# Loading streamed expert weights by whole thirds, into a ring of 15 places, three transfers under way

## Chip, cores and metric

The kernel runs on one core of one Trainium2 chip. The metric is the time of the program on the device in microseconds (us); lower is better. The times of a kernel are given as the median of its runs. One more execution is recorded by the hardware profiler, and all rows below come from that one.

## What is computed

One encoder layer over 1024 tokens of width 1024: windowed attention and a short gated convolution, joined by gates, then a mixture of 32 experts. Each token goes to one of four groups and there to two of eight experts. Only the last part concerns us here:

```python
def expert_block(args):
    xb, e = args
    hid = jax.nn.silu(xb @ w_gate[e]) * (xb @ w_up[e])
    return hid @ w_down[e]
...
y = y_pad[dest] * gates[order][:, None].astype(h.dtype)
out = jnp.zeros((t, d), h.dtype).at[tok].add(y)
```

The weights of one expert are 1024x256 (gate), 1024x256 (up) and 256x1024 (down) in float32, 3 MB, and 32 experts have 96 MB. All of them are used once.

## The kernel before

The program does norm, projections and attention, then the gates and the merge of both branches, then the experts. The experts' part (`phase_moe`, L1177 and after) takes the last 300 us of the span.

**An expert.** For expert e, GpSimd gathers up to 96 rows of the normed tokens from HBM into `xg` (L1121, an indirect DMA). TensorE turns them (`px`, L1132), ScalarE and VectorE split them into a high and a low part (`xT`), TensorE forms gate and up in one bank (`pgu`, 24 matmuls of 512 columns), ScalarE and VectorE form the hidden rows, TensorE turns them (`ph`, L1158) and multiplies by the down weights (`py`, 12 matmuls). ScalarE scales the result into `y` (L1170, two instructions), and GpSimd adds those rows to `out` in HBM (L1173, an indirect DMA that accumulates). There are two buffers `y`, the two halves of place 5, taken in turn; two `xg`; the accumulating transfers are ordered one behind the other, since they write the same tensor.

**The weights.** Host code lays them out as 96 thirds of 128 partitions x 2048 floats (1 MB, 8 KB a partition), numbered p = 0 to 95 in the order in which the kernel takes them: the gate and up weights are two thirds of an expert, its down weights the third one. A third has two halves s = 0, 1 (512 KB, 4 KB a partition). Each half, when it has come, is split once more, by ScalarE (L1107, high part) and VectorE (L1108, low part), into one of six places `wh` from which TensorE reads; `used()` issues these splits as TensorE lets go of a half. When VectorE has split a half, its place in the ring is free.

**The ring.** The first sixteen thirds (p below 16) are loaded whole or, for p = 12 and 13, as two halves into tiles of their own (`raw`), while merge and routing still run. From p = 16 on, the stream goes round the same memory. Thirds 16 and 17 go whole into places 2 and 0 (`WHOLE = 18`). From third 18 on, loads are halves into `slots`: the halves of places 2, 0, 1, 3, 4, 6, 7 to 15 in this order (place 5 serves as `y`) and one further half of its own, `more`, put in as number four, 31 halves in all. So a streamed half waits for the half 31 before it to be split, and by a dependency added by hand for the half four before it to have landed (`DEPTH = 4`): at most four halves, 2 MB, are under way. All loads are issued by SP's queue in order, but for the half (18, 1), which GpSimd's queue issues behind the gathers of experts 0 and 1 (`behind` only orders, it doesn't wait).

**Order.** ScalarE and VectorE run in the order of the program text in `phase_moe`: expert e's steps are woven with those of e - 1 and e + 1. The gather for expert e + 2 is issued when `xg` of expert e has been turned.

Of the kernel before, what the change touches and what calls it, by code (L numbers as in the profile page):

```python
# [8 lines left out]
F32 = mybir.dt.float32  # L9
# [8 lines left out]
P = 128  # L18
# [9 lines left out]
NE = 32  # L28
FF = 256
CAP = 96  # L30
LATE = (60, 94, 94)
WHOLE = 18
DEPTH = 4
TAP = 512
FILL = (4, 3, 4)

# [9 lines left out]
class Builder:  # L46
# [533 lines left out]

    def load(self, p, s=0):

        whole = p not in (12, 13) and p < WHOLE
        if (p, s) in self.loads:
            return
        if p in (0, 10, 14):
            pair = self.act(f"we{p}", {0: 3, 10: 4, 14: 1}[p], [2, 2048], F32)
            self.raw[p], self.raw[p + 1] = pair[:, 0], pair[:, 1]
        elif p in (12, 13):
            self.raw[p, s] = self.wpool.tile([P, 1024], F32, name=f"we{p}_{s}", tag="whl", bufs=4)  # L590
        elif p < 16 and p not in self.raw:
            tag = ("A0", "A1", "A2", "A3", "araw0", "craw0", "araw1", "craw1")[p - 2]
            self.raw[p] = (self.rawA if p < 6 else self.rawp).tile([P, 2048], F32, name=f"we{p}", tag=tag)
        elif p >= 16 and whole:
            self.raw[p] = self.raw[(2, 0)[p - 16]]
        j = self.order[p]
        to, sl = (self.raw[p], slice(0, 2048)) if whole else (self.half_of(p, s), slice(s * 1024, (s + 1) * 1024))
        q = self.nc.gpsimd if (p, s) == (18, 1) else self.nc.sync
        ins = q.dma_start(to, self.T["we"][j // 3, j % 3, :, sl])
        self.loads[p, s] = ins  # L600
        if whole:
            self.loads[p, 1] = ins
        if p == 15:
            self.behind(ins, self.wrote)
        if (p, s) == (18, 1):
            self.behind(ins, self.gathered)
        elif p > 18:
            dep = mybir.DependencyInfo(mybir.DependencyClass.Sync, mybir.DependencyReason.DATA)
            h = 2 * p + s - DEPTH
            self.tc.add_manual_dep(ins.ins, self.loads[h // 2, h % 2].ins.name, dep, reason="depth")  # L610

    def load_here(self, p):

# [2 lines left out]

    def half_of(self, p, s):

        if p in (12, 13):
            return self.raw[p, s]  # L620
        if p < 16:
            return self.raw[p][:, s * 1024:(s + 1) * 1024]
        return self.slots[(2 * p + s - 32) % len(self.slots)]

    def merge_consts(self, st):
        nc, T = self.nc, self.T
# [550 lines left out]
    def phase_moe(self, st):  # L1177
        nc, T = self.nc, self.T
        xp = self.pool("x6", stack=st)
        xts = [xp.tile([P, KT, 2, CAP], F32R, name="xT0")]  # L1180
        xgs = [xp.tile([P, D], F32, name=f"xg{i}") for i in range(2)]
        self.moe_pools(st, 0, 0)
        xts.append(self.sp6.tile([P, KT, 2, CAP], F32R, name="xT1"))
        for s in range(2):
            self.load(15, s)
        for s in range(2):
            self.half(1, s)
        self.nexth, self.free = 6, 0
        run = [self.expert(e, lambda c, s, e=e: self.w[3 * e + c, s], self.used, xgs[e % 2], xts[e % 2],
                           lambda e=e: self.slots[0] if e == NE - 1 else self.half_of(5, e % 2),  # L1190
                           self.idx[:CAP, 1, e:e + 1], self.gr[:CAP, 0, e:e + 1], self.gr[:CAP, 1, e:e + 1])
               for e in range(NE)]

        def start(e):
            next(run[e])
            if e + 2 < NE:
                self.gather(xgs[e % 2], self.idx[:CAP, 0, e + 2:e + 3])

        for e in range(2):
            self.gathered = self.gather(xgs[e], self.idx0[:CAP, e:e + 1])  # L1200
        order = [(p, s) for p in [2, 0, 1] + list(range(3, 16)) for s in range(2)]
        self.slots = [self.half_of(*h) for h in order if h[0] != 5]
        self.slots.insert(4, self.sp6.tile([P, 1024], F32, name="more"))
        for p in range(17, 19):
            for s in range(2):
                self.load(p, s)
        start(0)
        st.enter_context(self.tc.manual_schedule(engines={mybir.EngineType.Activation, mybir.EngineType.DVE}))
        for e in range(NE):
            next(run[e])  # L1210
            if e > 0:
                next(run[e - 1])
            if e + 1 < NE:
                start(e + 1)
            next(run[e])
            if e > 0:
                next(run[e - 1])
        next(run[-1])
        next(run[-1])
# [114 lines left out]
```

## Time and profile before

| | |
|---|---|
| Median of three runs | 977.77 us (977.6 to 978.74) |
| Profiled execution: its own time, its span | 980.05 us, 977.8 us |
| TensorE, busy share of the span | 97% (949.3 us) |
| VectorE, ScalarE, GpSimd | 75%, 60%, 12% |
| HBM read, written | 166.55 MB, 29.36 MB |
| DMA busy, last 12 of 40 slices | 9 tenths or more in 10 of them |
| Weight loads by SP's queue | 159 of 512 KB, 16 of 1024 KB |

The 40 slices of the page are 24.4 us each. TensorE shows nine tenths or more in nearly all of them, and so do the 16 DMA engines from slice 29 on, the experts' part. Shares over the whole span say little: the two meet only there, and the waits must be read by stretch. The DMA share of a stretch is the mean over 16 engines, and since transfers of neighbouring stretches are counted with where they start, it can read a few hundredths over 1.

### The profile page before, as it was taken

How to read it: one execution, taken by the hardware profiler on the slowest of the kernel's cores; microseconds unless marked ns; L12 is line 12 of the kernel's file. 1: busy time of each engine (PE TensorE's matmuls, PEld its weight loads, DVE VectorE, ACT ScalarE, POOL GpSimd, SP SyncE). 2: the span in 40 equal slices, each digit the busy share in tenths (PEclk: the TensorE clock that was granted, in tenths of full speed). 3: DMA queues.
4: the chain of work that ended last, by engine and by line, in shares of the span. 5: the costliest groups of instructions: out<-in, count | busy, mean ns of one | idle time of the engine just before them, and what ended most of it. 6: DMA issues, size and time to landing. Idle time of an engine off the chain costs nothing. (4 is left out here: it accounts for less than half of the span.)

```text
span 977.8 us, 13838 instructions
## 1 busy us (share of the span) xinstructions
PE 949.3 (97%) x4649; PEld 750.3 (77%) x4649; DVE 736.3 (75%) x1407; ACT 582.7 (60%) x1039; POOL 115.2 (12%) x90
## 2 busy tenths in 40 slices
PE   8999999999999999999999999979999999999993
PEld 5888888888878888888888888856777777777662
DVE  5777777878779656568765786478999999999882
ACT  4644555555544433346344435447999999899872
POOL 2222000000000000000000000013333232232211
PEclk9999999999999999999999999989999999999997
DMA  7201101000114233317677988768999999999993
GB/s 252 91 12 60 41 30 33 33 23 22 34 57 170 80 118 109 119 44 234 198 258 240 345 302 307 233 218 255 330 346 340 338 335 352 342 326 341 329 355 68
DMA packets 82749, 188.76 MB, mean 193 GB/s; under 512 B 10924, under 2 KB 28076, under 8 KB 80628
## 3 DMA queue, kind: packets, MB, share of 16 engines
q1 hardware_dynamic: 54772, 153.93, 45.3%
q0 software_dynamic: 7312, 17.60, 8.0%
q10 hardware_dynamic: 20592, 16.32, 5.0%
q8 instruction: 37, 0.61, 0.3%
q14 instruction: 36, 0.29, 0.1%
HBM read 166.55 MB, written 29.36 MB: 200 GB/s over the span
## 5 line engine op out<-in xcount | busy, mean ns | idle before, releaser
L1108 DVE TENSOR_TENSOR wh<-we,wh 128x1024 fp32r<-128x1024 f32 x186 | 219.8, 1217 | 29.7 <-ACT wh L1107 29.7
L1107 ACT ACTIVATE wh<-we 128x1024 fp32r<-128x1024 f32 x186 | 189.4, 1056 | 15.3 <-DMA we<-we 7.7
L70 PE MATMUL pgu<-wh,xT 128*96 128x512 f32 x768 | 190.5, 396 | 0.2 <-ACT xT L59 0.2
L70 PEld LDWEIGHTS pgu<-wh,xT 128*96 128x96 f32 x768 | 121.3, 161 | 49.9 <-ACT xT L59 0.4
L70 PE MATMUL py<-wh,hT 128*96 128x512 f32 x384 | 95.3, 395 | 3.8 <-DVE hT L60 2.0
L70 PEld LDWEIGHTS py<-wh,hT 128*96 128x96 f32 x384 | 61.4, 161 | 32.7 <-DVE hT L60 3.4
L70 PE MATMUL pc<-hT,wc_0s 128*128 128x512 f32 x288 | 77.5, 397 | 0.0
L70 PE MATMUL pc<-hT,wc_1s 128*128 128x512 f32 x288 | 75.8, 396 | 0.0
L1173 POOL DMA_INDIRECT out<-we,idx x32 | 52.6, 1644 | 183.0 <-ACT we L1170 127.4
L82 POOL TENSOR_TENSOR rstd_x<-ms_x,mhalf 128x1 f32<-128x1 f32 (+1 forms) x10 | 6.5, 651 | 573.7 <-DMA h2n<-rows 453.1
L70 PE MATMUL pq<-wq,hT 128*128 128x512 f32 (+1 forms) x384 | 71.2, 342 | 0.9 <-POOL wq L60 0.6
L70 PEld LDWEIGHTS pq<-wq,hT 128*128 128x128 f32 x384 | 59.5, 190 | 10.2 <-ACT hT L59 1.1
L70 PEld LDWEIGHTS pc<-hT,wc_1s 128*128 128x128 f32 x288 | 52.5, 188 | 9.3
L59 ACT ACTIVATE pT<-pp 128x512 fp32r<-128x512 f32 x44 | 26.1, 595 | 55.7 <-PE pp L425 55.7
L70 PEld LDWEIGHTS pc<-hT,wc_0s 128*128 128x128 f32 x288 | 52.1, 188 | 8.8 <-DVE wc_0s L60 0.3
L70 PE MATMUL po<-M,wo_1s 128*128 128x512 f32 x192 | 46.7, 391 | 0.0
L70 PE MATMUL po<-M,wo_0s 128*128 128x512 f32 x192 | 46.2, 390 | 0.0
L410 ACT ACTIVATE s<-s,nm 128x384 f32<-128x384 f32 (+1 forms) x64 | 36.9, 578 | 12.4 <-DVE nm L404 8.2
L70 PEld LDWEIGHTS po<-M,wo_1s 128*128 128x128 f32 x192 | 36.0, 188 | 8.8 <-DVE M L60 0.4
L70 PEld LDWEIGHTS po<-M,wo_0s 128*128 128x128 f32 x192 | 36.0, 188 | 7.5
L1121 POOL DMA_INDIRECT xg<-h2n,idx x32 | 35.9, 1122 | 47.7 <-PE px L1132 34.1
L1170 ACT ACTIVATE we<-py,gr 96x512 f32<-96x512 f32 x64 | 39.9, 672 | 2.4 <-PE py L70 2.4
(430 smaller groups left out, 1747.6 us busy)
## 6 DMA issues: line engine op xcount, KB each, us to landing
we<-we SPq DMA_DIRECT2D x153, 512.0 KB, 7.3
we<-we SPq DMA_DIRECT2D x16, 1024.0 KB, 7.0
sgl<-sgd SPq DMA_DIRECT2D x32, 256.0 KB, 3.6
x<-x SPq DMA_DIRECT2D x8, 512.0 KB, 4.2
wg_0r<-wcol SPq DMA_DIRECT2D x16, 256.0 KB, 2.8
wg_1r<-wcol SPq DMA_DIRECT2D x16, 256.0 KB, 2.7
wo_0r<-wo SPq DMA_DIRECT2D x16, 256.0 KB, 3.3
wo_1r<-wo SPq DMA_DIRECT2D x16, 256.0 KB, 3.6
```

The costliest lines, as they stand in the source:

```text
L59: a = self.nc.scalar.activation(hi, src, AF.Copy)
L70: return self.nc.tensor.matmul(*a, **k, skip_group_check=onto)
L82: self.powed = nc.gpsimd.tensor_tensor(out=r, in0=ms, in1=self.mhalf[:, :n], op=ALU.pow)
L410: ex = nc.scalar.activation(s[:, i, :nk], s[:, i, :nk], AF.Exp, bias=nm[:, i:i + 1], accum_out=sm[:, i:i + 1])
L1107: a = self.nc.scalar.activation(hl[:, 0], src, AF.Copy)
L1108: v = eng.tensor_tensor(out=hl[:, 1], in0=src, in1=hl[:, 0].bitcast(F32), op=ALU.subtract)
L1121: return self.nc.gpsimd.indirect_dma_start(out=xg[:CAP], out_offset=None, in_=self.h2n, in_offset=off, bounds_check=S, oob_is_err=False)
L1170: nc.scalar.activation(y[:C, c * 512:(c + 1) * 512], pys[c][:C], AF.Copy, scale=gate)
L1173: nc.gpsimd.indirect_dma_start(out=T["out"], out_offset=off, in_=y[:C], in_offset=None, bounds_check=S - 1, oob_is_err=False, compute_op=A ...
```

## The change

Streamed thirds are whole from p = 16 on, except where the place is 12 or 13, whose two tiles lie apart and stay halves. The ring is now 15 places of a third, in the order 2, 0, 1, 3, 4, 6 to 15; the extra half `more` is gone. A load waits for the whole third 15 before it to be split, and for the third three before it to have landed, so three thirds, 3 MB, may be under way. Third 18 is issued whole by GpSimd's queue. The last expert's `y`, which was `slots[0]`, the first half of place 2, is now named as that half.

```diff
-WHOLE = 18
-DEPTH = 4
+DEPTH = 3
+PLACES = (2, 0, 1, 3, 4, 6, 7, 8, 9, 10, 11, 12, 13, 14, 15)
...
     def load(self, p, s=0):
-        whole = p not in (12, 13) and p < WHOLE
+        whole = self.place(p) not in (12, 13)
...
         elif p >= 16 and whole:
-            self.raw[p] = self.raw[(2, 0)[p - 16]]
+            self.raw[p] = self.raw[self.place(p)]
...
-        q = self.nc.gpsimd if (p, s) == (18, 1) else self.nc.sync
+        q = self.nc.gpsimd if p == 18 else self.nc.sync
...
-        if (p, s) == (18, 1):
+        if p == 18:
             self.behind(ins, self.gathered)
         elif p > 18:
             dep = mybir.DependencyInfo(mybir.DependencyClass.Sync, mybir.DependencyReason.DATA)
-            h = 2 * p + s - DEPTH
-            self.tc.add_manual_dep(ins.ins, self.loads[h // 2, h % 2].ins.name, dep, reason="depth")
+            self.tc.add_manual_dep(ins.ins, self.loads[p - DEPTH, s].ins.name, dep, reason="depth")
+
+    def place(self, p):
+        return p if p < 16 else PLACES[(p - 16) % len(PLACES)]
...
     def half_of(self, p, s):
+        p = self.place(p)
         if p in (12, 13):
             return self.raw[p, s]
-        if p < 16:
-            return self.raw[p][:, s * 1024:(s + 1) * 1024]
-        return self.slots[(2 * p + s - 32) % len(self.slots)]
+        return self.raw[p][:, s * 1024:(s + 1) * 1024]
...
-                           lambda e=e: self.slots[0] if e == NE - 1 else self.half_of(5, e % 2),
+                           lambda e=e: self.half_of(2, 0) if e == NE - 1 else self.half_of(5, e % 2),
...
-        order = [(p, s) for p in [2, 0, 1] + list(range(3, 16)) for s in range(2)]
-        self.slots = [self.half_of(*h) for h in order if h[0] != 5]
-        self.slots.insert(4, self.sp6.tile([P, 1024], F32, name="more"))
```

No other engine's instructions change their order. On SP's queue, at the start of the streamed loads, there stood (`we_5207` is the pair of places 0 and 1, `we_4753` place 3, `lev` the routing's last value; 128x1024 is a half, 128x2048 a third):

```order
L599 DMA we_5207<-we 128x2048 [waits DMAHW4_49]
L599 DMA we_5207<-we 128x1024 [waits DMAHW4_49,DMAHW5_49,DVE_49,Activation_49]
L1224 TENSOR_LOAD lev [waits DVE_49]
L1224 ISA x2
L599 DMA more<-we 128x1024 [waits DVE_49,DMAHW6_49,PE_49,Pool_49]
L599 DMA we_4753<-we 128x1024 [waits DMAHW7_49,DVE_49]
L599 DMA we_4753<-we 128x1024 [waits DMAHW6_49,DMAHW0_49,DVE_49]
```

The rows are third 17, then the halves (19, 0), (18, 0), (19, 1) and (20, 0). Now, with `we_4919` place 4 and `we_5638` place 6, there stands:

```order
L599 DMA we_5207<-we 128x2048 [waits DMAHW4_49]
L1223 TENSOR_LOAD lev [waits DVE_49]
L1223 ISA x2
L599 DMA we_4753<-we 128x2048 [waits DMAHW5_49,DVE_49]
L599 DMA we_4919<-we 128x2048 [waits DMAHW6_49,DMAHW4_49,DVE_49]
L599 DMA we_5638<-we 128x2048 [waits DMAHW7_49,DMASW2_49,DVE_49]
```

These are thirds 17, 19, 20 and 21: third 19 now starts in place 3 rather than in the second half of place 1, and two issues of halves ahead of it are gone from this queue. On GpSimd's queue the one row that differs is the load behind the first two gathers, `we_5207<-we`, 128x1024 before and 128x2048 now.

## Rows read from the trace of the kernel before

**Rows 1.** Busy us by engine, granted clock, DMA share, GB/s, by stretch.
```profile
core 0: us, PE busy (x) PEld busy (x) DVE busy (x) ACT busy (x) POOL busy (x), PEclk, DMA share, GB/s
880.00:900.00 20.00, 20.00 (x101) 14.38 (x100) 18.64 (x23) 18.66 (x27) 5.02 (x4) 1.00 1.03 339
920.00:940.00 20.00, 17.88 (x88) 11.90 (x87) 15.45 (x19) 16.16 (x24) 3.92 (x3) 1.00 1.03 338
940.00:960.00 20.00, 18.76 (x89) 12.83 (x87) 17.42 (x21) 16.94 (x24) 3.74 (x2) 1.00 0.87 307
```

**Rows 2.** Waits of PE and ACT, 900 to 978: us in total, times, longest.
```profile
PE py L70 <- DVE hT L60: 2.0, 3, 0.8
PE py L70 <- ACT hT L59: 1.8, 2, 0.9
...
ACT wh L1107 <- DMA we<-we: 7.7, 7, 1.9
```

**Rows 3.** Timeline, PE: second dozen of gate and up matmuls, four neighbouring experts.
```profile
913.34 3.01 PE L70 MATMUL pgu<-wh,xT 128*96 128x512 f32 x12
...
922.52 2.99 PE L70 MATMUL pgu<-wh,xT 128*96 128x512 f32 x12
...
932.77 3.01 PE L70 MATMUL pgu<-wh,xT 128*96 128x512 f32 x12
...
944.01 3.02 PE L70 MATMUL pgu<-wh,xT 128*96 128x512 f32 x12
```

**Rows 4.** Waits of SP's queue: first row 660 to 680, second 800 to 900.
```profile
SPq L599 <- DVE wh L1108: 14.0, 5, 5.1
...
SPq L599 <- DMA we<-we: 77.3, 53, 3.2
```

**Rows 5.** Short stretches: thirds alone (first row), halves alone, both indirect transfers beside (last).
```profile
653.20:654.80 1.60, 1.32 (x13) 1.17 (x11) 0.24 (x2) 0.34 (x1) 0.00 (x0) 0.82 1.00 425
702.00:704.50 2.50, 2.50 (x17) 1.88 (x15) 2.50 (x5) 2.50 (x5) 2.19 (x2) 1.00 1.04 406
711.00:713.40 2.40, 2.40 (x18) 1.83 (x16) 2.40 (x6) 2.35 (x5) 2.09 (x2) 1.00 1.04 415
...
715.00:720.00 5.00, 5.00 (x24) 3.49 (x23) 4.29 (x5) 5.00 (x6) 0.78 (x1) 1.00 1.04 302
```

**Rows 6.** Timeline, SP issuing halves; VectorE splitting halves, 680 to 689.
```profile
681.26 0.33 SPq L599 DMA_DIRECT2D we<-we  x1
...
687.09 0.33 SPq L599 DMA_DIRECT2D we<-we  x1
...
680.02 4.71 DVE L1108 TENSOR_TENSOR wh<-we,wh 128x1024 fp32r<-128x1024 f32 x4
...
685.85 2.35 DVE L1108 TENSOR_TENSOR wh<-we,wh 128x1024 fp32r<-128x1024 f32 x2
```

**Rows 7.** Timeline: GpSimd's accumulating transfers; ScalarE writing `y` of experts 2 and 4.
```profile
701.10 2.17 POOL L1173 DMA_INDIRECT out<-we,idx  x1 [5.73 <-ACT wh L1107]
...
710.53 1.89 POOL L1173 DMA_INDIRECT out<-we,idx  x1 [5.98 <-ACT wh L1107]
...
698.50 1.24 ACT L1170 ACTIVATE we<-py,gr 96x512 f32<-96x512 f32 x2
...
716.86 1.24 ACT L1170 ACTIVATE we<-py,gr 96x512 f32<-96x512 f32 x2
```

**Rows 8.** Accumulating transfers, start to landing: 690 to 790, 790 to 900, 940 to 978.
```profile
DMA to landing us min/median/max: 7.7/8.5/8.9
...
DMA to landing us min/median/max: 6.7/7.2/8.5
...
DMA to landing us min/median/max: 4.6/5.4/7.3
```

**Rows 9.** ScalarE-queue stores of 256 KB to `out`, start to landing: 503 to 546, 610 to 640.
```profile
DMA to landing us min/median/max: 3.8/5.5/7.4
...
DMA to landing us min/median/max: 3.7/3.9/5.7
```

## The prediction

> **What bounds the kernel now.** I read the page first: the granted clock is full, and only in the experts' part do TensorE and the DMA engines both show nine tenths. So the views by stretch come next [rows 1]. From 880 to 900 TensorE is busy for all of 20.00 us, the DMA share is 1.03 and the clock 1.00: two resources without a gap. From 920 to 940 TensorE has 17.88, from 940 to 960 18.76. The waits of that end say why [rows 2]: TensorE waits 2.0 + 1.8 us for the hidden rows, which VectorE and ScalarE deliver late, and ScalarE itself stood 7.7 us, seven times, at a weight half that had not landed; before 900 it has no such wait. The timeline shows what that costs [rows 3]: the second dozen of gate and up matmuls starts 9.18 us after that of the expert before, then 10.25, then 11.24. Against a pace of 9.18 that is 1.07 + 2.06 = 3.1 us, and the last experts bring it to the 3.8 us of the waits.
>
> So TensorE sets the pace nearly to the end, the ring is drained meanwhile, since weights come more slowly than they are used, and at about 908 it is empty. **What a faster stream can win is those 3.8 us, not more**: behind them stands TensorE. SP's queue tells when which limit rules [rows 4]. From 660 to 680 it waits 14.0 us for VectorE to free a place (ring full); from 800 to 900 it waits 77.3 us in 53 pieces for a landing (four halves under way). With a share over 1 no engine idles for want of transfers, so more under way adds nothing by itself.
>
> **The change part by part.** The sum is made in the profiled span of 977.8 us (that execution's own time was 980.05); what it gives is put on the median of 977.77.
>
> *Larger rows.* Where only weights move, halves go at 406 and 415 GB/s and thirds at 425 [rows 5]. With 411 as the mean, two halves take 1,048,576 B / 411 = 2.55 us, a third 2.47: 0.08 us saved. Thirds 18 to 95 are 78, ten of them in places 12 and 13 and unchanged. The ring runs empty near third 84; of thirds 22 to 84, 55 are whole, so 55 x 0.08 = 4.4 us if the rate always held. But with the indirect transfers beside them the engines move 302 GB/s at the same share, so there something else may limit. The mean of 339 [rows 1] lies between 411 and 302 as for 0.34 of the time alone. That gives bounds of 0.34 x 4.4 = 1.5 and 4.4 us. I take 3.0, the middle, since neither row is nearer.
>
> *A shorter ring at the start.* Until about 688 the ring is the limit, and a third waits for both halves of its place. At 681.2 VectorE has split the second half of third 6; before, SP then issued (22, 0) [rows 6], now third 21. At 687.1 it was (24, 0), now 23. Just after such an issue the stream is one half behind, just before it two. A half costs 524,288 / 411 = 1.28 us, so the weights start their race 1.3 to 2.6 us later; I take 2.0. The engines make no use of the gap: at the ring's limit they have nothing to fetch.
>
> *Whole landings.* ScalarE can split the first half of a third only when the second has landed too. When the ring is empty that is 1.28 us later for every first half, while second halves come as before; a split takes about 1.06 us, so most of it is absorbed by order. Bounds 0 and 1.28; I take 0.5, as two halves are wanted one right behind the other.
>
> *Three under way.* 3 MB for 2 MB. Nothing idles [rows 1], so zero; what it could cost is under the rivals. *Fewer issues* on SP's queue (0.33 us each [rows 6]) cost nothing, as SP waits most of the time. *Third 18 on GpSimd's queue* is one issue instead of one; it waits for the second half of place 1 rather than the first, one split or 1.2 us (4.71 / 4 [rows 6]) later. Queued behind it on GpSimd is the gather for expert 2, which TensorE wants only after two experts; that hides it, and without that cover it would cost the 1.2 us.
>
> Sum: weights come 3.0 - 2.0 - 0.5 = 0.5 us earlier where they are late, and TensorE gets about as much back: 977.77 - 0.5, so **977.3 us**. With the bounds set against me: 1.5 - 2.6 - 1.28 = -2.4, 980.2; for me: 4.4 - 1.3 - 0 = 3.1, 974.7. About 0.2%, or 2 us, is what a measurement of this kernel can tell from no change: the forecast lies within it.
>
> **The rivals.**
>
> *The accumulating transfers become the bound (slower).* They go one behind the other. The transfer that starts at 701.10 is followed by one at 710.53, though `y` of expert 2 was written by 699.7 [rows 7]; between 690 and 790 one takes 8.5 us from start to landing [rows 8], with 0.8 to the next start 9.3: just over TensorE's pace of 9.18. The wait is put down to ScalarE's split, which had long been done, so it is the transfer before that ended it. GpSimd has no slack there and runs 1.4 us behind. After 790 it has 9.18 - 7.2 - 0.8 = 1.2. All of these share the engines with the weights: with few of them left, one takes 4.6 to 5.4 [rows 8]. Now every row of weights beside it is twice as long. What the trace shows of that: stores of the same size take 5.5 us beside whole thirds, 3.9 without most of them [rows 9]. A transfer has up to six rows for each of 16 engines; if each lets one row of weights pass, that is 8192 B instead of 4096 at 425 / 16 GB/s, 0.154 us more, and 0.9 for six. Bounds: 0, and 1.6 from the stores. It decides from here: `y` of expert 4 is begun at 716.86, the transfer of expert 2 from the same buffer lands at about 709.6, so 7.2 us of lateness can pile up before ScalarE, and then TensorE, waits. Eleven transfers up to 790 pile it up at 0.65 us each. Below that nothing happens; by 0.9 it costs 9.9 - 7.2 = 2.7 us. At 1.5, the fifth transfer reaches the limit, 6 x 1.5 + 17 x 0.3 = 14 us follow, and the 3.8 of late weights vanish: 988. Of 96 rows asked for, 2048 assignments over 32 experts fill 64 on the average, four for an engine: I take 4 x 0.154 = 0.6. That is so near 0.65 that this rival is strong. **988 us, chance 0.25.**
>
> The Trainium skill bears on this place. Its page "DMA: Bandwidth & Descriptors", section "Queues, rings and completion order", says that each engine takes turns between the queues that have work, a packet at a time. The two stretches of stores agree with it in direction (5.5 for 3.9 us), and no row shows the turns themselves. By that rule with a packet of one row, the 0.9 of above holds and the time would be about 977.77 + 2.7 - 0.5, or 980.
>
> *The weights are no longer late (faster).* If 3 MB under way, or whole contiguous thirds, also speed up the stretches with indirect transfers, from 302 GB/s by a few per cent, all waits of the end go, and TensorE bounds. 977.77 - 3.8 gives **974.0, chance 0.18**. For it: 302 at a share of 1.04 is far under 411. Against it: at that share a deeper queue has no idle engine to fill.
>
> The same page's section "Rules for kernel authors" asks for at least 1 MiB in each DMA for the best bandwidth, against 512 KB here. The rows do not show a loss of that kind, since 406 to 415 GB/s for halves is within 5% of 425. By the rule the time would be this rival's.
>
> *The larger rows bring nothing (about the same or slower).* If 425 against 411 is only the place in the program, the later start and the whole landings remain: 977.77 + 2.0 + 0.5 = **980.3, chance 0.10**. The ring order doing nothing at all is not a case: the issues of SP have changed.
>
> **How the numbers follow.** Forecast 0.47, transfers 0.25, no longer late 0.18, rows worthless 0.10. Faster by over 0.2%: 0.18 and 0.02 from the edge of the forecast, 0.20. Slower: 0.25, 0.07 of the last case and 0.02 from the forecast's other edge, 0.34. The same: 0.46. The range goes from 973.4, somewhat under the case in which all late weights go, to 989, which holds a little over half of the transfers' case; about 0.16 is left out, mostly above. The forecast's own range is 974.7 to 980.2.
>
> **What would show it.** Right: ScalarE's wait for weights at the end falls from 7.7 us to some 6 and still starts near 908; TensorE's pace stays 9.18 until then; alone, weights move at about 425 GB/s; the accumulating transfers' landing between 690 and 790 rises from 8.5 to no more than 9.1. The later start shows in SP waiting longer for VectorE until 690. Wrong: landings of 9.5 or more, with ScalarE waiting before L1170 and TensorE's pace over 9.3 in the middle of the experts' part (transfers); no wait for weights at all (faster); the wait starting before 900 (rows worthless).

## The result and the profile after

The changed kernel takes 984.27 us (median of five runs) against 977.77: ratio 1.0064, interval 1.0046 to 1.0082. It is slower by 6.5 us. The profiled execution took 986.3, with a span of 984.1. It lies 2.0 above its median, as that of the kernel before (980.05) lies 2.3 above its own, so the two spans compare like the medians.

The view by stretch shows where, over the same two stretches in both kernels (columns as in [rows 1]). Of the kernel before:

```profile
690.00:790.00 100.00, 100.00 (x503) 72.09 (x502) 92.38 (x110) 93.70 (x131) 32.40 (x22) 1.00 1.03 341
790.00:900.00 110.00, 110.00 (x553) 79.25 (x552) 100.85 (x120) 101.58 (x144) 30.63 (x24) 1.00 1.03 340
```

Of the changed kernel:

```profile
690.00:790.00 100.00, 100.00 (x503) 72.08 (x502) 92.69 (x110) 93.71 (x132) 32.35 (x21) 1.00 1.03 360
790.00:900.00 110.00, 104.65 (x511) 74.63 (x510) 93.34 (x110) 93.57 (x133) 36.07 (x23) 0.98 1.02 355
```

Up to 790 nothing is lost, and the engines move 360 GB/s instead of 341, at the same DMA share of 1.03. From 790 to 900 TensorE lacks 5.35 us, where before it lacked none. The waits from 690 to 945 name two causes, and neither is a weight (us in total, times, longest; [rows 2] is the view of before, from 900 on, where all its waits for weights lie):

```profile
ACT we L1172 <- DMA out<-we,idx: 9.4, 10, 1.9
PE px L1134 <- DMA xg<-h2n,idx: 7.3, 8, 1.9
```

ScalarE waits ten times before it writes `y` (line 1172 now), because an accumulating transfer still reads that buffer, and TensorE waits eight times for gathered rows. ScalarE's 7.7 us of waits for weights [rows 2] have no row any more. The landings of the accumulating transfers, 690 to 790 and 790 to 900, answer to the first two of [rows 8]:

```profile
DMA to landing us min/median/max: 8.2/9.3/10.5
...
DMA to landing us min/median/max: 8.7/9.1/10.0
```

With 0.8 us from a landing to the next start, 9.3 and 9.1 are periods of 10.1 and 9.9 us against TensorE's 9.18. The first five transfers, experts 0 to 4, still start within 0.6 us of their `y`. Their landings (680 to 720):

```profile
DMA to landing us min/median/max: 7.7/8.5/8.8
```

So even on time the period is 9.3, over the pace, and once they are late it is longer still. The timeline of GpSimd shows the chain, that of ScalarE the moment at which it bites (start, duration, line, idle time before and what ended it):

```profile
698.86 1.45 POOL L1175 DMA_INDIRECT out<-we,idx  x1 [5.27 <-ACT we L1172]
...
737.88 2.06 POOL L1175 DMA_INDIRECT out<-we,idx  x1 [6.98 <-ACT hT L59]
...
767.50 2.28 POOL L1175 DMA_INDIRECT out<-we,idx  x1 [7.35 <-ACT wh L1109]
...
789.36 2.59 POOL L1175 DMA_INDIRECT out<-we,idx  x1 [7.05 <-ACT wh L1109]
800.05 1.44 POOL L1175 DMA_INDIRECT out<-we,idx  x1 [6.66 <-DMA out<-we,idx]
...
938.85 1.44 POOL L1175 DMA_INDIRECT out<-we,idx  x1 [6.61 <-ACT we L1172]
```

```profile
789.10 1.25 ACT L1172 ACTIVATE we<-py,gr 96x512 f32<-96x512 f32 x2
...
799.61 0.69 ACT L1172 ACTIVATE we<-py,gr 96x512 f32<-96x512 f32 x1 [1.24 <-DMA out<-we,idx]
```

These are the transfers of experts 2, 6, 9, 11, 12 and 26. `y` of expert 12 (the first row of ScalarE) is done at 790.35, and its transfer starts at 800.05, 9.7 us late. The second row is `y` of expert 13, held up for 1.24 us by the transfer of expert 11: the first such wait. From 800.05 to 938.85 are 14 experts in 138.80 us, 9.91 each: the chain has become the pace, 0.73 us an expert over TensorE's own. The gathers stand behind the late transfers on GpSimd's queue and come late with them.

The sum is made from the first `y` to the last. Before, of the kernel now, and of the run below that leaves the transfers out, the last writing of `y`:

```profile
962.76 1.38 ACT L1170 ACTIVATE we<-py,gr 96x512 f32<-96x512 f32 x2 [2.42 <-PE py L70]
```

```profile
968.81 1.38 ACT L1172 ACTIVATE we<-py,gr 96x512 f32<-96x512 f32 x2 [2.42 <-PE py L70]
```

```profile
957.80 1.38 ACT L1172 ACTIVATE we<-py,gr 96x512 f32<-96x512 f32 x2 [2.41 <-PE py L70]
```

The first `y` begins at 680.15, 678.98 and 679.36. So the experts take 282.61 us before, 289.83 now and 278.44 without the transfers. Over that floor, in these executions, the kernel before loses 4.2 us to late weights, the changed one 11.4 to late transfers: 7.2 more, less 1.2 that its part began earlier, is the 6.3 between the spans, to 0.3.

### The profile page after: what moved, and what is told of

Read it like the earlier page. It is cut to its first block, busy times and chain, and to the rows that moved or that the text cites. A ratio compares the mean times of both kernels' runs of the same rounds, so it can differ in the third digit from the quotient of the medians.

```text
span 984.1 us, 13576 instructions
## 1 busy us (share of the span) xinstructions
PE 950.4 (97%) x4649; PEld 750.9 (76%) x4649; DVE 736.5 (75%) x1407; ACT 583.1 (59%) x1039; POOL 128.0 (13%) x90
## 5 line engine op out<-in xcount | busy, mean ns | idle before, releaser
L1110 DVE TENSOR_TENSOR wh<-we,wh 128x1024 fp32r<-128x1024 f32 x192 | 226.3, 1217 | 34.6 <-ACT wh L1109 33.5
L1109 ACT ACTIVATE wh<-we 128x1024 fp32r<-128x1024 f32 x192 | 194.2, 1054 | 9.2 <-DVE O L927 4.7
L1175 POOL DMA_INDIRECT out<-we,idx x32 | 55.6, 1737 | 190.2 <-ACT we L1172 107.0
L1123 POOL DMA_INDIRECT xg<-h2n,idx x32 | 45.6, 1426 | 33.8 <-PE px L1134 16.0
```

Of the source, the lines that this page charges most:

```text
L1109: a = self.nc.scalar.activation(hl[:, 0], src, AF.Copy)
L1110: v = eng.tensor_tensor(out=hl[:, 1], in0=src, in1=hl[:, 0].bitcast(F32), op=ALU.subtract)
L1123: return self.nc.gpsimd.indirect_dma_start(out=xg[:CAP], out_offset=None, in_=self.h2n, in_offset=off, bounds_check=S, oob_is_err=False)
L1175: nc.gpsimd.indirect_dma_start(out=T["out"], out_offset=off, in_=y[:C], in_offset=None, bounds_check=S - 1, oob_is_err=False, compute_op=A ...
```

## The experiments

Each is timed beside the kernel before; that one's medians were 977.3 to 977.7.

**Short rows in long loads.** Everything of the change stays but the length of a row (`we2` holds the same weights, each third as two blocks of 128 x 1024):

```diff
-        ins = q.dma_start(to, self.T["we"][j // 3, j % 3, :, sl])
+        src = self.T["we"][j // 3, j % 3, :, sl]
+        if whole and p > 18:
+            to = to.rearrange("p (s f) -> p s f", s=2)
+            src = self.T["we2"][j // 3, j % 3].rearrange("s p f -> p s f")
+        ins = q.dma_start(to, src)
```

> The changed kernel with one thing undone: thirds 19 to 95 are still one load of 1 MB each, into the same 15 places, three under way, but their rows are 4 KB (a second copy of the weights in HBM holds each third as two halves one behind the other, so a partition's 8 KB come from two places). Theory 1, the longer rows: each accumulating transfer lets an 8 KB row pass where it let a 4 KB row pass; that took them from 8.5 to 9.3 us and over TensorE's pace. Then here the landing falls back to 8.3 to 8.8 us between 690 and 790, no wait of ScalarE for a transfer of `out` is left, and the time is 977 to 980. Theory 2, the depth or the ring: three thirds under way or the later start lengthen the transfers. Then the landing stays at 9.2 or more and the time at 983 to 986.

Measured: 975.99 us, ratio 0.9989 (0.9973 to 1.0005). No wait of ScalarE for a transfer, none of TensorE for gathered rows. The landings in the same two stretches, each with the durations of GpSimd's own instruction (ns, min/median/max) and with what ended its idle time before most of them:

```profile
L1179 POOL DMA_INDIRECT out<-we,idx x11: 1437/1442/1449, 690.2 to 783.1; - x11
...
  ACT we L1176: 54.3, 10
...
DMA to landing us min/median/max: 6.9/7.8/9.1
```

```profile
L1179 POOL DMA_INDIRECT out<-we,idx x12: 1437/2060/2481, 792.4 to 895.5; - x12
...
  ACT wh L1113: 46.2, 8
...
DMA to landing us min/median/max: 7.7/8.5/9.5
```

All of the loss is gone with the row length alone; the ring, the depth, the loads of 1 MB and the landings by thirds have stayed. Theory 1 holds, and time and landing came out below its ranges (977 to 980, 8.3 to 8.8). The rows also show something new: in the first stretch ten of eleven transfers start as soon as `y` is written (`ACT we`), in the second most start late (the releaser named is a split long done, as in [rows 7]), and the late ones take 0.7 us longer. Most of that, 0.6 us, lies in GpSimd's own instruction: 1.44 us on time, 2.06 late. The kernel before has the same pair: late by some 1.4 us it took 8.5, on time 7.2 [rows 8]. Why the instruction takes longer is not shown; the next gather starts while the transfer is under way in both cases.

**Rows of 2 KB.** The same with `s=4` and blocks of 128 x 512.

> As the run with 4 KB rows (one load of 1 MB for each third, 15 places, three under way), with rows of 2 KB: a third dose. If each row of an accumulating transfer lets rows of weights pass in turn, its landing goes on falling: 9.3 us at 8 KB and 7.8 at 4 KB between 690 and 790 make 7.0 to 7.5 at 2 KB. If the turns are not by rows, it stays at 7.8 or rises. The weights move more slowly if a row costs something by itself; if they stay over 57 MB between 700 and 900 they are not late and the time is 974 to 978, else up to 982.

Measured: 981.25 us, ratio 1.0033 (1.0017 to 1.0049). The landing is 7.4 us in both stretches, in the range expected, but the weights are late again:

```profile
ACT wh L1113 <- DMA we<-we: 9.8, 8, 2.4
```

GB/s between 790 and 900 fall to 339, at a DMA share of 1.04 (349 at 4 KB, 1.03). So 9.3, 7.8 and 7.4 us for rows of 8, 4 and 2 KB (the first mostly late, the others on time): the transfers gain ever less from shorter rows, and the weights lose. 4 KB lies between the two losses.

**Two thirds under way.**

```diff
-DEPTH = 3
+DEPTH = 2
```

> The changed kernel with two thirds under way instead of three (2 MB, as much as the four halves of before); rows stay 8 KB. Theory 1, the longer rows: the landing between 690 and 790 stays at 9.2 us or more and ScalarE waits before `y` for about 8 us or more in all; the time is 983 to 986. Theory 2, the depth: the landing falls to some 8.5, the waits go and the time is 977 to 980.

Measured: 990.55 us, ratio 1.0128 (1.0100 to 1.0157). Both theories missed: the landing fell to 8.3 and 6.7 us, and ScalarE never waited for a transfer, but the weights were late by more than in any other run. The waits from 690 to 945, and the first of the two stretches:

```profile
ACT wh L1109 <- DMA we<-we: 19.1, 10, 2.7
```

```profile
690.00:790.00 100.00, 100.00 (x503) 72.08 (x502) 92.40 (x110) 93.72 (x132) 29.61 (x21) 1.00 1.00 328
```

The DMA share is 1.00 with 328 GB/s, not 1.03 with 360: two loads move less, and the transfers land sooner beside them. So the long rows lengthen the transfers with three under way; how much they would at the same rate with two, this run can't say. It says that the depth carries the rate.

**Six halves under way in the kernel before** (4 KB rows, 31 halves in the ring):

```diff
-DEPTH = 4
+DEPTH = 6
```

> The kernel before with one number changed: six halves under way instead of four (3 MB instead of 2 MB, as in the changed kernel); rows of 4 KB, ring of 31 halves. Theory A: what took the late weights away in the run with 4 KB rows is the depth, and the longer rows are what harms. Then ScalarE's 7.7 us of waits for weights at the end fall under 2, weights move at 350 to 362 GB/s between 720 and 900, the accumulating transfers land in 8 to 8.8 us and never stop ScalarE, and the time is 972 to 976. Theory B: the depth gives nothing, and it was the single load of 1 MB: the rates stay at 335 to 347 GB/s and the time at 977 to 978. Theory C: the deeper queue by itself lengthens the accumulating transfers over 9.2 us: ScalarE waits before `y` and the time is 979 or more.

Measured: 976.05 us, ratio 0.9988 (0.9974 to 1.0002). The first stretch and its landing:

```profile
690.00:790.00 100.00, 100.00 (x503) 72.09 (x502) 92.37 (x110) 93.72 (x132) 28.61 (x22) 1.00 1.04 355
```

```profile
DMA to landing us min/median/max: 7.2/7.7/8.6
```

From 690 to 945 there is no wait for weights, for a transfer or for a gather, and the experts take 278.44 us from the first `y` to the last, the floor to 0.01. Theory A holds: 341 becomes 355 GB/s by depth alone, and depth alone does not lengthen the transfers (7.7 us, under the 8 to 8.8 expected). Its profiled span, 973.1, is the shortest of all that keep the transfers, 4.7 under that of the kernel before. By the medians the gain is only 1.6 us, and the interval reaches no change. The profiled execution of the kernel before may well have had more late weights than its usual one; the next run suggests it too.

**A ring of 30 halves in the kernel before.**

```diff
-        self.slots.insert(4, self.sp6.tile([P, 1024], F32, name="more"))
```

> The kernel before without the tile `more`: a ring of 30 halves instead of 31, all else as it was. It prices the shorter ring alone. The prediction's term says that a ring that is one to two halves shorter starts the weights 1.3 to 2.6 us later; here it is one half, so ScalarE's waits at the end grow from 7.7 us and the time is 1 to 1.5 us more, 978.5 to 979.5. If the start is not what decides, the time is that of before within 0.5 us.

Measured: 979.24 us, ratio 1.0019 (1.0003 to 1.0034): 1.6 us slower (the interval: 0.3 to 3.3), where one half at the prediction's price is 1.28. Its profiled execution lies under its median (span 974.3), and ScalarE's waits for weights, which should have grown from 7.7 us, were 4.2 in it. So the profile does not show the loss; the medians alone carry it, and how late the weights are changes from one execution to the next. Its landings, 7.6 and 7.2 us, are those of six halves within 0.2: with short rows the depth doesn't matter to them.

**Without the accumulating transfers**, in both kernels:

```diff
+        if e in ("m", 0, NE - 1):
             nc.gpsimd.indirect_dma_start(out=T["out"], out_offset=off, in_=y[:C], in_offset=None,
```

> The changed kernel without the accumulating transfers of experts 1 to 30 (their rows are left out of the result; `y` is computed and written as ever). If these transfers carry the whole loss, TensorE's pace is 9.17 us to the end, ScalarE waits for nothing at `y`, TensorE's waits for gathered rows vanish, weights are never late, and the time is 970 to 974. If the loss lies in the weights (whole landings, the shorter ring) or the gathers, it stays above 977.

> The kernel before without the accumulating transfers of experts 1 to 30, as a control for the run before this one. Their share of the DMA engines goes to the weights, so the late weights vanish here too: 971 to 975. By the theory the changed kernel without them is as fast as this one within 1 us, so the order of the two kernels turns with the transfers; if the changed one is still 5 us slower, the theory falls.

Measured: 972.12 us, ratio 0.9948 (0.9931 to 0.9966), and 971.67, 0.9944 (0.9923 to 0.9964). The rows of experts 1 to 30 are missing from the result of both. With the transfers the kernels are 6.5 us apart, without them 0.4, which the intervals don't tell from none (the order, expected to turn, does not); both take 278.44 us from the first `y` to the last. So the transfers carry the whole difference. (Both also end some 4 us sooner behind the last `y`; 1.4 of that is the last transfer, which has no other ahead of it.) The first stretch, of the changed kernel and of the one before:

```profile
690.00:790.00 100.00, 100.00 (x504) 72.08 (x503) 92.37 (x111) 93.73 (x131) 12.56 (x11) 1.00 1.02 373
```

```profile
690.00:790.00 100.00, 100.00 (x503) 72.08 (x502) 92.37 (x111) 93.70 (x131) 12.53 (x11) 1.00 1.02 347
```

The larger and deeper stream is the faster one, as was intended; what it costs, it costs through the transfers.

**The gathers first, and a third buffer of `y`.** Three kernels: the gather for expert e + 5 ahead of the transfer of expert e; that with a third `y` in the room of `more`; the third `y` alone (`added_to` keeps the transfers by expert, `ymore` is a tile of 128 x 1024).

```diff
-                self.gather(xgs[e % 2], self.idx[:CAP, 0, e + 2:e + 3])
+                g = self.gather(xgs[e % 2], self.idx[:CAP, 0, e + 2:e + 3])
+                if e >= 3:
+                    self.behind(self.added_to[e - 3], g)
```

```diff
-                           lambda e=e: self.half_of(2, 0) if e == NE - 1 else self.half_of(5, e % 2),
+                           lambda e=e: self.half_of(2, 0) if e == NE - 1 else (self.half_of(5, 0), self.half_of(5, 1), ymore)[e % 3],
```

> The changed kernel with another order on GpSimd's queue: the gather for expert e + 5 stands ahead of the accumulating transfer of expert e, not behind it. The two buffers of `y` stay. Theory 1 says that the chain of accumulating transfers is the limit from expert 13 on, and that TensorE's 7.3 us of waits for gathered rows are its consequence: then these waits go, ScalarE's wait for the transfers before `y` grows to take their place, the transfers' period stays at 9.9 to 10.0 us, and the time is 982 to 985. Rival: the late gathers are what costs, since the gather stands behind a late transfer; then the time falls to 977 to 979.

> As the run before this one, and `y` has three buffers instead of two: the third is a tile of 4 KB a partition, the room that the removed tile `more` had. Theory 1: the transfers may now run up to 16 us behind instead of 7 to 10; with 0.7 to 0.9 us more behind at each expert, ScalarE first waits near expert 20 instead of 12, seven or eight experts at 0.75 us are won back, and the time is 976 to 980. If the lag of the transfers is not what stops TensorE (weights or splitting instead), the time stays at 982 to 986.

> The changed kernel with three buffers of `y` instead of two, the order on GpSimd's queue as it was. By the theory two limits stand close together: ScalarE's wait for a buffer of `y`, which this removes up to 16 us of lateness, and the gathers, which stand behind the late transfers and already kept TensorE 7.3 us. So lateness should grow to some 11 or 12 us and TensorE's waits for gathered rows should grow in the place of ScalarE's for `y`: the time is 981 to 985, little or nothing won. If only the buffers of `y` were the limit, the time falls to 976 to 979.

Measured: 991.29 us (ratio 1.0128, 1.0101 to 1.0155), 987.63 (1.0101, 1.0075 to 1.0128) and 984.78 (1.0076, 1.0053 to 1.0099). The waits for a transfer or a gather from 690 to 945, of the three in turn:

```profile
ACT we L1172 <- DMA out<-we,idx: 36.3, 17, 5.3
```

```profile
ACT we L1172 <- DMA out<-we,idx: 4.5, 5, 1.8
PE px L1134 <- DMA xg<-h2n,idx: 4.2, 6, 1.8
ACT more L1172 <- DMA out<-more,idx: 1.4, 2, 0.8
```

```profile
PE px L1134 <- DMA xg<-h2n,idx: 4.2, 7, 0.9
```

In the first, TensorE's waits for gathers are gone and ScalarE's have grown from 9.4 to 36.3 us, as theory 1 said; its time is 6 us over the range expected, because the order itself costs. The gather is free to go only when TensorE has turned the rows before it, so the first transfer starts at 685.78, 4.5 us behind its `y` (681.31), and ScalarE first waits at expert 6 instead of 13. The third buffer gives 3.7 us of that back (expected: about 5), but its time is 7.6 over the range expected, 976 to 980, presumably for the same reason. Alone it wins nothing, as expected: ScalarE's waits vanish, and TensorE still waits for gathers behind transfers that are 10 us late. Those waits were to grow from 7.3 us and fell to 4.2; this execution's TensorE was slower by itself (9.29 us an expert, see the last run), which gave the transfers 0.1 us more at each expert. Neither the buffer nor the order took the loss away; while the chain's period is over the pace they only move the wait.

**Long rows up to third 48, then halves**, six of them under way:

```diff
-        whole = self.place(p) not in (12, 13)
+        whole = self.place(p) not in (12, 13) and p <= 48
```

> The changed kernel with rows of 8 KB only up to third 48; thirds 49 to 95 come as two loads of halves each, with rows of 4 KB, into the same places, still three thirds (six halves) under way. The theory says that lateness of the accumulating transfers piles up and costs nothing below some 7 to 9 us. The last long third is on its way near 760; by then the transfers ran 4 to 6 us behind in the changed kernel. So here they should reach 4 to 7 us near expert 9 and stay or fall after that, ScalarE should not wait before `y` at all, weights should not be late, and the time should be 974 to 977. If a few long rows are enough to stop TensorE, or the transfers stay over 9.2 us with the short rows behind them, the time is over 979.

Measured: 977.94 us, ratio 1.0002 (0.9987 to 1.0017). The mechanism went as expected: the transfer of expert 11 (788.10) starts 5.5 us behind its `y` (782.56), the largest lag, from there it falls to 2 or 3, and nothing waits for a transfer, a gather or a weight. The time is 0.9 us over the range expected, and TensorE's pace in the profile was 9.29 us, not 9.18, which also gave the transfers 0.1 us more at each expert: see the next run.

**The run with 4 KB rows once more.**

> The run with 4 KB rows once more, for one question: there TensorE's pace was 9.28 us an expert instead of 9.17, its matmuls in the experts' part started 236 ns apart instead of 232, and nothing waited. If this belongs to the layout (rows of a load that come from two places), it is 9.28 again; if it belonged to that one execution, it is 9.17 here and the time some 3 us less.

Measured: 976.34 us in one run, span 974.1 against 976.2; the transfers land in 7.7 and 8.3 us, and again neither ScalarE nor TensorE waits for them. The gate and up matmuls between 700 and 790, in the first execution and in this one (busy us, mean ns of one):

```profile
L70 PE MATMUL pgu<-wh,xT 128*96 128x512 f32 x234 | 58.7, 399 | 0.0
```

```profile
L70 PE MATMUL pgu<-wh,xT 128*96 128x512 f32 x234 | 58.0, 396 | 0.0
```

The slower pace belonged to the execution, not to the kernel. The span fell by 2.1 and not by 3; here ScalarE waited again for weights at the end, 3.0 us in all.

## Why the prediction was wrong

The prediction took 977.3 us for the likeliest; the case that came is its first rival, the accumulating transfers (988, chance 0.25), and the measured 984.27 lies between the two, slower and not the same.

- **What bounds, and the cap: held in the profiled execution.** TensorE's pace and late weights at the end; without them 4.2 us of the experts' time go (282.61 to 278.44, predicted 3.8). But that execution took 2.3 us more than the median to which the sum was applied, and by the medians ending the late weights gave 1.6 us, not clear of no change. So 3.8 stood for that execution.
- **Three under way, 0: the step that failed on the faster side.** "With a share over 1 no engine idles" was read from [rows 1]. Six halves in the kernel before move 355 GB/s where four move 341, at nearly the same share (1.04 and 1.03). That alone ends the late weights in the profile, so the term was not 0 but the whole price of them. A share near 1 doesn't say that a deeper queue can bring nothing.
- **Larger rows, -3.0:** at equal depth, rows of 8 KB give 360 GB/s, rows of 4 KB 354 to 359 (690 to 790). That is 0.3 to 1.7%. The 3.0 us taken are 1.8% of the 170 us that 55 thirds take at 339 GB/s, so the term stands at or over the upper end. Once the depth had ended the late weights, there was nothing left for it to win.
- **Shorter ring, +2.0, and whole landings, +0.5:** the first came out at 1.6 us for one half by the medians (0.3 to 3.3), where late weights bound; its profile does not show it. In the changed kernel weights are never late, so neither term acts.
- **Third 18, fewer issues: 0** as said; no wait points there.
- **The forecast's premise, that the transfers stay under 0.65 us more each: the step that failed and decided.** The working gave 0.6 from four rows, 0.9 from six, 1.6 from the stores beside whole thirds [rows 9], and the smallest was taken. Like against like, the longer row costs 0.8 to 1.0: late, from 8.5 in the kernel before to 9.3; on time, in the first five transfers, from 7.5 with short rows (first run with 4 KB) to 8.5. So the 0.9 of six rows had the size, and the 0.6 of four, which was taken, was too small; 1.5 us, from 7.8 to 9.3, is row and lateness together, and the prediction had no term for the lateness. The point from which it decides was right: ScalarE first waited, for 1.2 us, on a transfer that started 8.2 us late, which makes a limit of 7.0; predicted 7.2.
- **The rival's size, 988:** from 790 on it used 7.2 us plus 1.5, a period 0.3 over the pace. The transfers stayed late there and took 9.1, so the period was 0.73 over it, for 14 experts; in turn the first stretch added some 0.75 each (8.2 us by expert 11), not 1.5. The two errors partly cancel, 11.4 us lost for 14 predicted, each less the late weights: that 988 came near is in part luck.
- **Weights no longer late (974.0):** they aren't late, as this rival said, but the transfers are.
- **The signs:** ScalarE waiting before `y` and a pace over 9.3 (9.9 from 800 on) were the rival's signs, and both came. The landing, 9.3, was over the 9.1 that the forecast allowed and under the 9.5 that the rival named, which was set too high.

On the two rules that were weighed: the Trainium skill, "DMA: Bandwidth & Descriptors", section "Queues, rings and completion order", has engines take turns between queues, a packet at a time, and gives a packet as typically 9 to 17 descriptors. The turns agree with the runs (9.3, 7.8 and 7.4 us for 8, 4 and 2 KB). The packet doesn't, if a row is one descriptor: by an estimate from that page's figure nine rows, each 0.154 us longer, in each of six turns would make 8 us more, and 0.8 to 1.0 was measured, nearer to one row a turn. The turns themselves no run shows. The section "Rules for kernel authors" of the same page of the Trainium skill asks for at least 1 MiB in each DMA for the most bandwidth. The runs do not agree at 2 MB under way: loads of 1 MB moved 328 GB/s and loads of 512 KB 341. At 3 MB it was 360 and 355. Here the amount under way told more than the size of a load.

## What to carry to other kernels

Before a stream's rows are made longer, look for whoever shares the engines with it, above all for a chain of small transfers that runs one behind the other, and compare its period (landing plus restart) with the pace of the work that feeds it. Where the period comes over the pace (here from 8.6, landing 7.8 and restart 0.8, with short rows to 9.3 with long ones, against 9.18, on time), the difference piles up until the buffers are used, and more buffers only put that off. Try the depth of the queue by itself first: here one number ended the late weights that the larger loads were to end, with rows that left the transfers alone. And a price read from one profiled execution is the price of that execution: compare its time with the median first.

## What was not expected of the hardware

- **A DMA share of 1 or more does not say that no more can be moved.** 328, 341, 355 and 360 GB/s were moved from 690 to 790 at shares of 1.00, 1.03, 1.04 and 1.03.
- **A late accumulating transfer takes longer than one on time:** 8.5 against 7.8 us with rows of 4 KB, 8.5 against 7.2 in the kernel before, 9.3 against 8.5 in the changed one. So lateness feeds itself there. With two thirds under way there is no such difference (by the trace, late 7.0 and on time 7.6 us for experts 1 to 23). A good part lies in GpSimd's own instruction (2.06 against 1.44 us); why is open.
- **TensorE has two paces in this part.** In three profiled executions (the first with 4 KB rows, long rows first, three buffers of `y`) the gate and up matmuls took 399 ns on the mean and an expert 9.28 to 9.29 us, in the others 396 or 397 ns and, where nothing waits, 9.18, at a granted clock of 1.00 from 690 to 790 in both. The same kernel showed both. What chooses is open; it is some 3 us of the time (281.69 against 278.44 us from the first `y` to the last), and may be part of the spread between runs.
